# Head of an expert layer: token tile 0 ahead of tile 1, GpSimd out of the routing, weights in order of use, last norm's row by a broadcast load

## The chip, the cores and the metric

The kernel runs on one core of a Trainium2 chip. The metric is the time of one execution on the device in microseconds; the smaller is the better. Times are medians of repeated runs; the profile is of one execution, with its own time.

## The reference

A two-part network on 256 tokens of width 1024, all in float32. The first part has a pooling mixer, two gated feed-forward layers (width 2816) and a block attention of 16 heads. The second part is one hybrid layer: a modulation from a vector c (six rows: shift, scale, gain for the mixer and for the experts), a sparse attention and an RWKV branch that are mixed by sigmoid gates and projected by w_out, and then a mixture of experts. The change lies from the end of the mix on, which computes:

```python
x = x + g1 * (mixed @ w_out)
h2 = rms_norm(x, norm2_g) * (1 + sc2) + sh2
x = x + g2 * moe_ffn(h2, router_w, router_bias, exp_gate, exp_up, exp_down, sh_gate, sh_up, sh_down)
return rms_norm(x, final_g)
```

moe_ffn takes sigmoid scores of 64 experts per token, adds a bias for the choice, keeps the best 4 of 8 groups (by the sum of each group's two best), takes the best 8 experts in them, and weights them by their scores, normalised to a sum of 2.5. Each expert is a gated feed-forward of width 256; a shared expert of the same form runs on all tokens.

## The kernel before, in words

**Tiling.** The 256 tokens are two tiles of 128, called t = 0 and 1. The residual x_sb lies with tokens in the partitions. Sums over tokens by 1024 columns are built in four PSUM banks, accs[t][h], h being the half of 512 columns. [...]

**End of the mix** (lines 976 to 1025). `dense` runs the branch projections and the eight units of w_out. Each unit multiplies a split pair of operands (a high and a low part, three matmuls, `mm3` at line 205) into accs. The last `late` units (line 996, here two) are done for token tile 0 only, and `tail(h)` adds them for tile 1 afterwards, one half h at a time. `upd(t, h)` (line 1011) multiplies the sum by g1 and adds x_sb, two VectorE passes over 128x512, and ScalarE sums the squares. `rsq` (line 231) turns these into the norm's factor: two small VectorE operations and a power on GpSimd. From line 1018 on ScalarE, VectorE and TensorE run in the order in which the program is written (`manual_schedule`); GpSimd's and SyncE's order is set by the compiler's planner.

**Head of the experts** (`moe`, line 1351). `xnorm(t)` scales accs into xn, half on VectorE and half on ScalarE. TensorE transposes xn in eight 128x128 pieces for a tile, and VectorE (pieces 0 to 3) and ScalarE (4 to 7) write them with gain and shift to hT. The router's matmuls (line 1432) follow for both tiles, then one sigmoid, then `modrow(g2, 5)` (line 532), which spreads the gain row g2 over the partitions by eight matmuls and two ScalarE copies. xn is split into xH (ScalarE) and xL (GpSimd, line 1438). `shared_gu(jj)` (line 1444) is the shared expert's gate and up projection, 32 TensorE instructions, for one of two column halves; GpSimd multiplies the shared down weights by g2 (line 1452). Then VectorE routes, tile by tile (lines 1455 to 1479): maxima in groups, the groups' choice, the eight best, sel and the weights gw. From sel TensorE counts ranks (prk, lines 1482 to 1484), between shared_gu(0) and shared_gu(1).

**The loop over pairs of experts** (line 1645). 64 experts run as 32 pairs. Tokens are gathered by matmuls with one-hot matrices (`place`, `gather`, pxg), four experts at a time. For pair n: `gu(0)`, the first half of gate and up; `turn` of the pair before (transposing its activations to aT); `comb` of the pair before that (adding its result into accs); a part of the next gather; `gu(1)`; `act`; and `down(0)`, `down(1)` of the pair before. `down` multiplies by g2 on VectorE, rounds to yH on ScalarE, and keeps the rest in yL on VectorE. After the loop the last pair's turn, down and comb run, the squares are summed, and the final norm is written out.

**Weights.** All weights of `moe` go through a ring of NR = 18 slots of 1 MiB (`etile`), in three pools: ering1 (slots 0 to 8), ering2 (9 to 15), ering3 (16 and 17). A slot is reused when its last reader is done. A pair takes four slots for gate and up (`gload`) and two for down (`load_down`). xn and hT use the two slots of ering3 first, the shared gate, up and down slots 0 to 2. SyncE issues all these loads, one behind the other: its queue stands at a load whose slot isn't free. The row of the final norm takes a slot six pairs before the end (line 1648): a 4 KB load, spread to all partitions by matmuls (pbc, line 1654) and ScalarE copies.

**Pools.** The pool of the mix ("mix", g1row and temporaries) lies on the left side of SBUF among pools that close before ering3 and ering2 open.

Of the kernel before, what the change touches and what calls it, by code (L numbers as in the profile page):

```python
# [128 lines left out]
def build(ctx, tc, A, out, dbg=None):  # L129
# [680 lines left out]
    with ExitStack() as es:  # L810
# [169 lines left out]
        wk = open_pool(es, "mix")  # L980
# [15 lines left out]
        dn, tail = downs(A["w_out_2"][0], 8, lambda u: parts[u], accs, 2)  # L996
# [28 lines left out]
        upd(1, 1)  # L1025
    pa.close()
    ering3 = open_pool(ctx, "ering3", E3)
    ering2 = open_pool(ctx, "ering2", NR - E1 - E3)
    moe(ctx, nc, tc, A, out, x_sb, accs, xp, modrow, gcol, bcol, rt, K, ident, sm, ps,
# [321 lines left out]
def moe(ctx, nc, tc, A, out, x_sb, accs, xp, modrow, gcol, bcol, rt, K, ident, sm, ps,  # L1351
# [48 lines left out]
    with open_pool("route") as w2:  # L1400

        xns = etile(2, 1024, True)
        hT = etile(8, 256, True)
        xn = xns[:, 0, :], xns[:, 1, :]

        turned = lambda a: a.rearrange("n (p k) -> n k p", k=8)
        wide = lambda a, h: a.rearrange("n (k p) -> n k p", k=8)[:, :, 64 * h:64 * h + 64]
# [3 lines left out]
        def xnorm(t):  # L1411
            V.tensor_scalar(wide(xn[t], 0), turned(accs[t][0]), x2s[t], None, op0=OP.mult)
            S.activation(wide(xn[t], 1), turned(accs[t][1]), AF.Copy, scale=x2s[t])
        xnorm(0)
        x2s[1] = rsq(x2s[1], "n")
        xnorm(1)
        for t in range(2):
            for k4 in range(2):
                p = ps("pt")
                for kk in range(4):  # L1420
                    k = 4 * k4 + kk
                    PE.transpose(p[:, kk * 128:(kk + 1) * 128], xn[t][:, k * 128:(k + 1) * 128], ident)
                for kk in range(4):
                    k, c = 4 * k4 + kk, slice(kk * 128, (kk + 1) * 128)
                    if k4:
                        S.activation(hT[:, k, sl[t]], p[:, c], AF.Identity, scale=gc(k), bias=bc(k))
                    else:
                        V.tensor_scalar(hT[:, k, sl[t]], p[:, c], gc(k), bc(k), op0=OP.mult, op1=OP.add)
        p = ps("pr")
        for t in range(2):  # L1430
            for k in range(8):
                PE.matmul(p[:, t * 64:t * 64 + 64], hT[:, k, sl[t]], rtr[:, k, :], start=k == 0, stop=k == 7)
        S.activation(sc[:, :, 0, :], p[:, 0:128].rearrange("p (t e) -> p t e", t=2), AF.Sigmoid)
        V.tensor_tensor(sc[:, :, 1, :], sc[:, :, 0, :], rb[:, None, :].to_broadcast([128, 2, 64]), op=OP.add)
        modrow(g2, 5)
        for t in range(2):
            S.activation(xH[:, t, :], xn[t], AF.Copy)
            G.tensor_tensor(xL[:, t, :], xn[t], xH[:, t, :].bitcast(F32), op=OP.subtract)
# [5 lines left out]
        def shared_gu(jj):  # L1444
# [7 lines left out]
            G.tensor_tensor(down[:, jj, :], down[:, jj, :], g2, op=OP.mult)  # L1452
        shared_gu(0)
        sel = w2.tile([128, 2, 64], F32, name="sel")
        for t in range(2):
            s8 = w2.tile([128, 8, 8], F32, name="s8", bufs=2)
# [29 lines left out]
        V.scalar_tensor_tensor(rks.rearrange("p a b -> p (a b)"), p[:, 0:128], 1.0, sel.rearrange("p a b -> p (a b)"), op0=OP.add, op1=OP.mult)  # L1486

# [130 lines left out]
    for jj in range(2):  # L1618
        V.tensor_tensor(sa[:, jj, :], sa[:, jj, :], spg[jj][:, 256:512], op=OP.mult)
# [25 lines left out]
    for n in range(NE // 2):  # L1645
        g, i = divmod(n, NG // 2)
        more = g + 1 < NE // NG
        if n == NE // 2 - 6:
            fgt = etile(2, 1024)
            fg, frow = fgt[:, 0, :], fgt[0:1, 1, :]  # L1650
            DMA.dma_start(frow, A["final_g_2"][None, :])
# [126 lines left out]
```

## Time and profile before

| what | value |
|---|---|
| median of 3 runs | 1396.15 us (1391.35 to 1396.72) |
| profiled execution | 1396.91 us, span 1394.8 us |
| TensorE busy | 1338.2 us (96% of the span) |
| VectorE busy | 743.8 us (53%) |
| ScalarE busy | 548.3 us (39%) |
| GpSimd busy | 118.8 us (9%) |
| loads and stores | 361.38 MB, mean 259 GB/s |

The span is the profiled execution from its first to its last instruction; its own time has a few us around it. Engines are PE (TensorE), PEld (its weight loads, which overlap), DVE (VectorE), ACT (ScalarE), POOL (GpSimd) and SP (SyncE, which only issues loads here). [...] Busy shares are averages over parts with different limits; the part that the change touches begins at about 843 us of the span (the last branch projection is done), the pairs of experts run from 904 to about 1373, and the end follows.

### The profile page before, as it was taken

How to read it: one execution, taken by the hardware profiler on the slowest of the kernel's cores; microseconds unless marked ns; L12 is line 12 of the kernel's file. 1: busy time of each engine (PE TensorE's matmuls, PEld its weight loads, DVE VectorE, ACT ScalarE, POOL GpSimd, SP SyncE). 2: the span in 40 equal slices, each digit the busy share in tenths (PEclk: the TensorE clock that was granted, in tenths of full speed). 3: DMA queues.
4: the chain of work that ended last, by engine and by line, in shares of the span. 5: the costliest groups of instructions: out<-in, count | busy, mean ns of one | idle time of the engine just before them, and what ended most of it. 6: DMA issues, size and time to landing. Idle time of an engine off the chain costs nothing.

```text
span 1394.8 us, 22867 instructions
## 1 busy us (share of the span) xinstructions
PE 1338.2 (96%) x9151; PEld 1003.3 (72%) x9151; DVE 743.8 (53%) x1420; ACT 548.3 (39%) x1087; POOL 118.8 (9%) x158
## 2 busy tenths in 40 slices
PE   5999999999999998899999998899999999999996
PEld 4899997998799997789989888644545445445443
DVE  4656657565765555468777676533333343343333
ACT  4444445655544445365664543211221222222212
POOL 3010001000100002203342100300000000000000
PEclk9999999999999999899999998999999999999998
DMA  7887766652866646944411159499999999999993
GB/s 253 294 247 250 250 225 213 210 192 92 290 234 225 212 157 207 182 131 147 154 62 63 63 219 361 134 335 380 405 408 409 408 409 409 408 409 409 368 403 138
DMA packets 157312, 361.38 MB, mean 259 GB/s; under 512 B 9865, under 2 KB 92101, under 8 KB 153874
## 3 DMA queue, kind: packets, MB, share of 16 engines
q1 hardware_dynamic: 154674, 353.36, 70.0%
q0 software_dynamic: 2528, 6.51, 1.8%
q8 instruction: 75, 1.23, 0.4%
q14 instruction: 35, 0.29, 0.1%
HBM read 357.46 MB, written 2.37 MB: 258 GB/s over the span
## 4 chain that ended last, share of the span: by engine, by line
PE 79%; DMA 7%; issue 5%; DVE 5%; ACT 2%; POOL 1%; SPq 0%; POOLq 0%; ACTq 0%; DVEq 0%
PE pgu L1557 15%; PE pdn L1581 7%; PE pgu L206 5%; PE pgu L207 5%; PE pgu L208 5%; PE pxg L1524 4%; PE pz L206 4%; PE acc L1597 4%; PE pz L207 4%; PE pz L208 4%; PE acc L208 3%; PE acc L206 3%; PE acc L207 3%; DMA ew<-in_exp_up 3%; DMA raw<-in_w_gate_up 2%
## 5 line engine op out<-in xcount | busy, mean ns | idle before, releaser
L191 DVE TENSOR_TENSOR wL<-raw,wH 128x1024 fp32r<-128x1024 f32 (+1 forms) x229 | 270.7, 1186 | 200.2 <-ACT wH L190 199.4
L190 ACT ACTIVATE wH<-raw 128x1024 fp32r<-128x1024 f32 (+1 forms) x231 | 235.7, 1026 | 254.2 <-PE pgu L207 106.7
L207 PE MATMUL pgu<-hL,wH 128*128 128x256 f32 x704 | 198.1, 281 | 1.3 <-DVE hL L267 1.3
L206 PE MATMUL pgu<-hH,wH 128*128 128x256 f32 x704 | 198.0, 282 | 0.0
L208 PE MATMUL pgu<-hH,wL 128*128 128x256 f32 x704 | 198.0, 281 | 0.0
L207 PEld LDWEIGHTS pgu<-hL,wH 128*128 128x128 f32 x704 | 133.0, 189 | 3.5 <-DVE hL L267 1.7
L206 PEld LDWEIGHTS pgu<-hH,wH 128*128 128x128 f32 x704 | 132.7, 189 | 2.9 <-issue 0.6
L208 PEld LDWEIGHTS pgu<-hH,wL 128*128 128x128 f32 x704 | 133.0, 189 | 0.0
L206 PE MATMUL pz<-hH,wH 128*128 128x256 f32 x400 | 119.5, 299 | 3.3 <-ACT hH L190 2.6
L1557 PE MATMUL pgu<-ew,xx 128*64 128x512 f32 x512 | 117.8, 596 | 1.6 <-DMA ew<-in_exp_up 1.5
L1557 PE MATMUL pgu<-ew,xg 128*64 128x512 f32 x512 | 117.0, 596 | 0.4 <-DMA ew<-in_exp_up 0.4
L1581 PE MATMUL pdn<-ew,aT 128*64 128x512 f32 (+1 forms) x528 | 115.6, 580 | 0.0
L207 PE MATMUL pz<-hL,wH 128*128 128x256 f32 x400 | 114.3, 286 | 1.2 <-DVE hL L191 1.2
L208 PE MATMUL pz<-hH,wL 128*128 128x256 f32 x400 | 113.4, 284 | 0.0
L1581 PEld LDWEIGHTS pdn<-ew,aT 128*64 128x64 f32 x528 | 37.8, 137 | 72.1 <-issue 71.1
L1557 PEld LDWEIGHTS pgu<-ew,xx 128*64 128x64 f32 x512 | 36.2, 137 | 69.4 <-issue 66.1
L1557 PEld LDWEIGHTS pgu<-ew,xg 128*64 128x64 f32 x512 | 35.6, 137 | 67.4 <-issue 66.2
L1584 ACT ACTIVATE yH<-pdn 128x512 fp32r<-128x512 f32 (+1 forms) x66 | 38.5, 584 | 112.6 <-DVE pdn L1583 112.6
L206 PEld LDWEIGHTS pz<-hH,wH 128*128 128x128 f32 x400 | 76.6, 192 | 7.5 <-ACT hH L190 2.9
L207 PEld LDWEIGHTS pz<-hL,wH 128*128 128x128 f32 x400 | 76.7, 192 | 2.6 <-DVE hL L191 1.4
L208 PEld LDWEIGHTS pz<-hH,wL 128*128 128x128 f32 x400 | 76.6, 191 | 0.4 <-issue 0.3
L236 POOL TENSOR_TENSOR rstd<-ssv,mhalf 128x1 f32<-128x1 f32 x16 | 9.8, 614 | 768.0 <-DVE ssv L234 767.9
(408 smaller groups left out, 2528.1 us busy)
## 6 DMA issues: line engine op xcount, KB each, us to landing
ew<-in_exp_gate SPq DMA_DIRECT2D x128, 512.0 KB, 12.7
ew<-in_exp_up SPq DMA_DIRECT2D x128, 512.0 KB, 12.8
ew<-in_exp_down SPq DMA_DIRECT2D x64, 1024.0 KB, 12.1
raw<-in_w_gate_up SPq DMA_DIRECT2D x44, 1024.0 KB, 5.5
raw<-in_ada_w SPq DMA_DIRECT2D x24, 1024.0 KB, 5.0
raw<-in_w_in SPq DMA_DIRECT2D x23, 1024.0 KB, 5.3
raw<-in_w_down SPq DMA_DIRECT2D x22, 1024.0 KB, 5.3
raw<-in_w_kv SPq DMA_DIRECT2D x8, 1024.0 KB, 5.5
```

The source lines that it names most:

```text
L190: S.activation(dstH, src, AF.Copy)
L191: second.tensor_tensor(dstL, src, dstH.bitcast(F32), op=OP.subtract)
L206: PE.matmul(out_, lH, rH, start=first, stop=False)
L207: PE.matmul(out_, lH, rL, start=False, stop=False)
L208: PE.matmul(out_, lL, rH, start=False, stop=last)
L236: G.tensor_tensor(r, v, mhalf[:, 0:1], op=OP.pow)
L1524: PE.matmul(p[:, kk * w:kk * w + w], x[:, t, (kb + kk) * 128:(kb + kk) * 128 + 128], r, start=t == 0 and i == 0, stop=t == 1 and i == 1, s ...
L1557: PE.matmul(self.pg[64 * e:64 * e + 64, :].rearrange("p (i c) -> p i c", i=2), self.xg[:, k, 64 * e:64 * e + 64], self.W[e][k // 4][:, :, ...
L1581: PE.matmul(p[64 * e:64 * e + 64], self.aT[:, j, 64 * e:64 * e + 64], self.D[e][:, j, c:c + w], start=j == 0, stop=j == 1, skip_group_chec ...
L1584: S.activation(yH[:, sl], p, AF.Copy)
L1597: PE.matmul(self.ac[t][h][:, sl], l, self.y[h][i][:, sl], start=False, stop=i == 1 and self.last, skip_group_check=True)
```

## The change

- `late` is 4 instead of 2: four units of w_out are held back for token tile 1.
- The mix pool lies on the right side and closes after the last `upd`. ering3 opens earlier, xn is taken from it in `build`, and xnorm(0) runs ahead of upd(1, 1).
- In `moe`, token tile 0 is transposed, written to hT, and routed to its scores before tile 1 is transposed; modrow(g2, 5) stands ahead of the first router; the sigmoid runs tile by tile, as does the bias addition of the choice.
- xL is computed on VectorE after the ranks, and the shared down weights are multiplied by g2 on VectorE after `begin(0)`; both were GpSimd's.
- `load_down` of a pair is issued after the gate and up loads of the next pair.
- The final norm's row is loaded by one load that writes all 128 partitions, behind the last expert's weights; its matmuls and copies go.
- At the end, the last pair's turn stands between the two downs of the pair before, and its down(0) ahead of the older pair's combs; its down(1) comes ahead of its comb(0).

```diff
--- before.py
+++ after.py
@@ -977,7 +977,8 @@
         rt = open_pool(ctx, "router", side="right").tile([128, 576], F32, name="rt")
 
 
-        wk = open_pool(es, "mix")
+        mix = ctx.enter_context(ExitStack())
+        wk = open_pool(mix, "mix", side="right")
         g1 = wk.tile([128, D], F32, name="g1row")
         modrow(g1, 2)
         parts = {}
@@ -993,7 +994,7 @@
                     parts[2 * c + jj] = (mH[:, jj, :], mL[:, jj, :])
             return fin
         accs = []
-        dn, tail = downs(A["w_out_2"][0], 8, lambda u: parts[u], accs, 2)
+        dn, tail = downs(A["w_out_2"][0], 8, lambda u: parts[u], accs, 4)
         br = []
         wrb = loads(A["w_rwkv_br_2"][0], 4)
         for c in range(4):
@@ -1022,11 +1023,21 @@
         upd(1, 0)
         x2s[0] = rsq(x2s[0], "n")
         tail(1)
-        upd(1, 1)
+
+
     pa.close()
     ering3 = open_pool(ctx, "ering3", E3)
+    xn = ering3.tile([128, 2048], F32, tag="ew", name="ew").rearrange("p (t d) -> p t d", t=2)
+
+    def xnorm(t):
+        turned, wide = (lambda a: a.rearrange("n (p k) -> n k p", k=8)), xn[:, t, :].rearrange("n (k p) -> n k p", k=8)
+        V.tensor_scalar(wide[:, :, 0:64], turned(accs[t][0]), x2s[t], None, op0=OP.mult)
+        S.activation(wide[:, :, 64:128], turned(accs[t][1]), AF.Copy, scale=x2s[t])
+    xnorm(0)
+    upd(1, 1)
+    mix.close()
     ering2 = open_pool(ctx, "ering2", NR - E1 - E3)
-    moe(ctx, nc, tc, A, out, x_sb, accs, xp, modrow, gcol, bcol, rt, K, ident, sm, ps,
+    moe(ctx, nc, tc, A, out, accs, xn, xnorm, xp, modrow, gcol, bcol, rt, K, ident, sm, ps,
         x2s, order, rsq, hl, rows, bcast, ering1, ering2, ering3)
 
 
@@ -1348,7 +1359,7 @@
         yield
 
 
-def moe(ctx, nc, tc, A, out, x_sb, accs, xp, modrow, gcol, bcol, rt, K, ident, sm, ps,
+def moe(ctx, nc, tc, A, out, accs, xn, xnorm, xp, modrow, gcol, bcol, rt, K, ident, sm, ps,
         x2s, order, rsq, hl, rows, bcast, ering1, ering2, ering3):
     V, S, G, PE, DMA = nc.vector, nc.scalar, nc.gpsimd, nc.tensor, nc.sync
     NE, CAP, NG = 64, 64, 4
@@ -1398,44 +1409,42 @@
     bc = lambda k: bcol[:, 1, k:k + 1]
     g2 = mp.tile([128, D], F32, name="g2row")
     with open_pool("route") as w2:
-
-        xns = etile(2, 1024, True)
         hT = etile(8, 256, True)
-        xn = xns[:, 0, :], xns[:, 1, :]
-
-        turned = lambda a: a.rearrange("n (p k) -> n k p", k=8)
-        wide = lambda a, h: a.rearrange("n (k p) -> n k p", k=8)[:, :, 64 * h:64 * h + 64]
         sc = w2.tile([128, 2, 2, 64], F32, name="scn")
         sl = [slice(t * 128, (t + 1) * 128) for t in range(2)]
 
-        def xnorm(t):
-            V.tensor_scalar(wide(xn[t], 0), turned(accs[t][0]), x2s[t], None, op0=OP.mult)
-            S.activation(wide(xn[t], 1), turned(accs[t][1]), AF.Copy, scale=x2s[t])
-        xnorm(0)
+        def turns(t):
+
+            pt = [ps("pt") for _ in range(2)]
+            for k in range(8):
+                PE.transpose(pt[k // 4][:, k % 4 * 128:k % 4 * 128 + 128], xn[:, t, k * 128:(k + 1) * 128], ident)
+            return [p[:, kk * 128:(kk + 1) * 128] for p in pt for kk in range(4)]
+
+        def features(t, pt, ks):
+            for k in ks:
+                if k > 3:
+                    S.activation(hT[:, k, sl[t]], pt[k], AF.Identity, scale=gc(k), bias=bc(k))
+                else:
+                    V.tensor_scalar(hT[:, k, sl[t]], pt[k], gc(k), bc(k), op0=OP.mult, op1=OP.add)
+
+        def router(t):
+            p = ps("pr")
+            ks = (0, 4, 1, 5, 2, 6, 3, 7)
+            for k in ks:
+                PE.matmul(p[:, 0:64], hT[:, k, sl[t]], rtr[:, k, :], start=k == 0, stop=k == ks[-1])
+            S.activation(sc[:, t, 0, :], p[:, 0:64], AF.Sigmoid)
+
+        pt = turns(0)
+        features(0, pt, (0, 1, 4, 5, 6, 7))
         x2s[1] = rsq(x2s[1], "n")
+        features(0, pt, (2, 3))
         xnorm(1)
+        modrow(g2, 5)
+        router(0)
+        features(1, turns(1), range(8))
+        router(1)
         for t in range(2):
-            for k4 in range(2):
-                p = ps("pt")
-                for kk in range(4):
-                    k = 4 * k4 + kk
-                    PE.transpose(p[:, kk * 128:(kk + 1) * 128], xn[t][:, k * 128:(k + 1) * 128], ident)
-                for kk in range(4):
-                    k, c = 4 * k4 + kk, slice(kk * 128, (kk + 1) * 128)
-                    if k4:
-                        S.activation(hT[:, k, sl[t]], p[:, c], AF.Identity, scale=gc(k), bias=bc(k))
-                    else:
-                        V.tensor_scalar(hT[:, k, sl[t]], p[:, c], gc(k), bc(k), op0=OP.mult, op1=OP.add)
-        p = ps("pr")
-        for t in range(2):
-            for k in range(8):
-                PE.matmul(p[:, t * 64:t * 64 + 64], hT[:, k, sl[t]], rtr[:, k, :], start=k == 0, stop=k == 7)
-        S.activation(sc[:, :, 0, :], p[:, 0:128].rearrange("p (t e) -> p t e", t=2), AF.Sigmoid)
-        V.tensor_tensor(sc[:, :, 1, :], sc[:, :, 0, :], rb[:, None, :].to_broadcast([128, 2, 64]), op=OP.add)
-        modrow(g2, 5)
-        for t in range(2):
-            S.activation(xH[:, t, :], xn[t], AF.Copy)
-            G.tensor_tensor(xL[:, t, :], xn[t], xH[:, t, :].bitcast(F32), op=OP.subtract)
+            S.activation(xH[:, t, :], xn[:, t, :], AF.Copy)
 
         xx = xp.tile([128, 2, 8, 128], F32, name="xx", tag="x_sb")
         sa = xx[:, 0, 0:4, :].rearrange("p a b -> p (a b)").rearrange("p (j n) -> p j n", j=2)
@@ -1449,10 +1458,10 @@
                     PE.matmul(p[:, i * 256:(i + 1) * 256], w[:, k, jj * 128:(jj + 1) * 128], hT[:, k, :], start=k == 0, stop=k == 7,
                               skip_group_check=True)
             S.activation(sa[:, jj, :], p[:, 0:256], AF.Silu)
-            G.tensor_tensor(down[:, jj, :], down[:, jj, :], g2, op=OP.mult)
         shared_gu(0)
         sel = w2.tile([128, 2, 64], F32, name="sel")
         for t in range(2):
+            V.tensor_tensor(sc[:, t, 1, :], sc[:, t, 0, :], rb, op=OP.add)
             s8 = w2.tile([128, 8, 8], F32, name="s8", bufs=2)
             for g in range(8):
                 V.max(s8[:, g, :], sc[:, t, 1, g * 8:(g + 1) * 8])
@@ -1484,6 +1493,8 @@
         PE.matmul(p[:, 64:128], K("su"), sel[:, 1, :], start=False, stop=True)
         shared_gu(1)
         V.scalar_tensor_tensor(rks.rearrange("p a b -> p (a b)"), p[:, 0:128], 1.0, sel.rearrange("p a b -> p (a b)"), op0=OP.add, op1=OP.mult)
+        for t in range(2):
+            V.tensor_tensor(xL[:, t, :], xn[:, t, :], xH[:, t, :].bitcast(F32), op=OP.subtract)
 
     wk = ctx.enter_context(open_pool("moew"))
 
@@ -1616,6 +1627,7 @@
 
     begin(0)
     for jj in range(2):
+        V.tensor_tensor(down[:, jj, :], down[:, jj, :], g2, op=OP.mult)
         V.tensor_tensor(sa[:, jj, :], sa[:, jj, :], spg[jj][:, 256:512], op=OP.mult)
     half(0, 0)
     half(0, 1)
@@ -1645,17 +1657,10 @@
     for n in range(NE // 2):
         g, i = divmod(n, NG // 2)
         more = g + 1 < NE // NG
-        if n == NE // 2 - 6:
-            fgt = etile(2, 1024)
-            fg, frow = fgt[:, 0, :], fgt[0:1, 1, :]
-            DMA.dma_start(frow, A["final_g_2"][None, :])
-            for h in range(2):
-                p = ps("pbc")
-                PE.matmul(p, K("ones")[0:1, :], frow[:, h * 512:(h + 1) * 512], start=True, stop=True)
-                S.copy(fg[:, h * 512:(h + 1) * 512], p)
         pT, wsl = tiles[g]
         cur = Pair((2 * n, 2 * n + 1), spots[g % 2][:, i], pT[:, i, :], wsl[:, i:i + 1], accs, n > NE // 2 - 3)
-        cur.load_down()
+        if prev:
+            prev.load_down()
         if more and i == 0:
             begin(g + 1)
         cur.gu(0)
@@ -1672,14 +1677,20 @@
         cur.act()
         if prev:
             prev.down(0)
+            if n == NE // 2 - 1:
+                cur.turn()
             prev.down(1)
         old, prev = prev, cur
-    prev.turn()
+    prev.load_down()
+    fgt = etile(2, 1024)
+    fg, sq = fgt[:, 0, :], fgt[:, 1, :]
+    DMA.dma_start(fg, bcast(A["final_g_2"], D))
+    prev.down(0, 2)
     old.comb(0)
     old.comb(1)
     order.close()
     cnt = nc.values_load(mi[0:1, 0:1], min_val=0, max_val=T)
-    o, sq = etile(2, 1024), fgt[:, 1, :]
+    o = etile(2, 1024)
 
     def squares(t, h):
         S.activation(sq[:, h * 512:(h + 1) * 512], accs[t][h], AF.Square, accum_out=ss[t][:, h:h + 1])
@@ -1704,11 +1715,10 @@
     ss = [sm.tile([128, 2], F32, name="ss") for _ in range(2)]
     order = ctx.enter_context(ExitStack())
     order.enter_context(tc.manual_schedule(engines=MANUAL))
-    prev.down(0, 2)
+    prev.down(1, 2)
     prev.comb(0, 2)
     for t in range(2):
         squares(t, 0)
-    prev.down(1, 2)
     for t in range(2):
         gain(t)
     prev.comb(1, 2)
```

## Rows read from the trace of the kernel before

**Rows 1.** Busy by stretch: us, length, engines (x instructions), PEclk, DMA share, GB/s.

```profile
870.00:880.00 10.00, 9.25 (x48) 8.30 (x46) 9.31 (x36) 4.74 (x6) 7.35 (x4) 0.93 0.00 0
1100.00:1200.00 100.00, 100.00 (x515) 48.92 (x512) 38.25 (x73) 20.40 (x46) 0.00 (x0) 1.00 1.03 409
1300.00:1350.00 50.00, 49.59 (x249) 24.64 (x246) 17.41 (x32) 9.79 (x24) 0.00 (x0) 1.00 0.97 376
```

**Rows 2.** SyncE's queue: start, us, queue, line, operation.

```profile
857.85 0.34 SPq L1381 DMA_DIRECT2D ew<-in_exp_up  x1
881.94 0.33 SPq L1381 DMA_DIRECT2D ew<-in_exp_gate  x1
...
931.07 10.58 SPq L1366 DMA_DIRECT2D ew<-in_exp_down  x2
...
1307.57 9.64 SPq L1366 DMA_DIRECT2D ew<-in_exp_down  x2
...
1356.34 7.12 SPq L1366 DMA_DIRECT2D ew<-in_exp_down  x2
```

**Rows 3.** TensorE's timeline, head: start, us; in brackets idle before, releaser.

```profile
858.50 3.67 PE L1422 MATMUL pt<-k_base,ew 128*128 128x128 f32 x16 [3.79 <-ACT ew L1413]
861.96 6.93 PE L1432 MATMUL pr<-rt,ew 128*128 128x64 f32 x32
...
871.78 7.07 PE L1449 MATMUL pgu<-ew 128*128 128x256 f32 x32
...
882.87 0.69 PE L1484 MATMUL prk<-sel,k_base 128*128 128x64 f32 x2 [3.62 <-DVE sel L1474]
883.35 9.62 PE L1449 MATMUL pgu<-ew 128*128 128x256 f32 x32
...
904.14 3.65 PE L1557 MATMUL pgu<-ew,xg 128*64 128x512 f32 x16
```

**Rows 4.** VectorE's timeline, end of the mix and routing.

```profile
848.05 0.68 DVE L191 TENSOR_TENSOR mL<-mixt,mH 128x512 fp32r<-128x512 f32 x1
851.35 0.70 DVE L1013 TENSOR_TENSOR acc<-acc,g1row 128x512 f32<-128x512 f32 x1 [2.62 <-PE acc L208]
...
869.24 0.29 DVE L1434 TENSOR_TENSOR scn<-scn,rt 128x128 f32<-128x128 f32 x1 [6.51 <-ACT scn L1433]
...
872.83 2.22 DVE L1479 TENSOR_SCALAR gw<-gw,wr 128x64 f32<-128x64 f32 x1
...
883.31 0.25 DVE L1479 TENSOR_SCALAR gw<-gw,wr 128x64 f32<-128x64 f32 x1
```

**Rows 5.** GpSimd's timeline, routing.

```profile
872.65 4.67 POOL L1452 TENSOR_TENSOR ew<-ew,g2row 128x1024 f32<-128x1024 f32 x2 [13.72 <-ACT g2row L538]
```

**Rows 6.** Busy by stretch, TensorE alone: us, length, busy, PEclk, DMA, GB/s.

```profile
554.00:555.00 1.00, 0.00 (x0) 1.00 1.09 345
857.00:858.00 1.00, 0.00 (x0) 0.83 1.04 410
871.00:872.00 1.00, 1.00 (x8) 0.84 0.00 0
```

**Rows 7.** TensorE's timeline, an earlier pair of transposes.

```profile
555.06 1.06 PE L249 MATMUL pt<-k_base,xn 128*128 128x128 f32 x8 [1.66 <-DVE xn L773]
```

**Rows 8.** The chain that ended last, in the loop: start, us, what.

```profile
1281.73 1.91 PE pbc L1654 x4
```

**Rows 9.** TensorE's timeline, end of the loop.

```profile
1360.26 3.62 PE L1557 MATMUL pgu<-ew,xx 128*64 128x512 f32 x14 [1.52 <-DMA ew<-in_exp_up]
...
1369.50 3.60 PE L1581 MATMUL pdn<-ew,aT 128*64 128x512 f32 x16
```

**Rows 10.** The tile psrow: its load's time from issue to landing.

```profile
DMA to landing us min/median/max: 10.6/10.6/10.6
```

**Rows 11.** VectorE's timeline, the end.

```profile
1375.49 0.41 DVE L1570 COPY aT<-pat 128x256 f32<-128x256 f32 x1
...
1383.66 1.29 DVE L1688 TENSOR_TENSOR ew<-acc,ew 128x512 f32<-128x512 f32 x2
```

## The prediction

> **What bounds the kernel now.** I read the busy time by stretch first. The expert part, from 904 us on, shows two resources full at once: TensorE busy in all of 1100 to 1200, and the loads at 409 GB/s [rows 1]. One pair of experts is 6 MiB, 6.29 MB: at 409 GB/s that is 15.4 us, while TensorE takes (1369.5 - 904.1) / 32 = 14.5 us a pair [rows 3, 9]. The loads are the slower of the two, TensorE lives on what was loaded ahead, and at the last pair the lead is gone: it waits 1.52 us for in_exp_up [rows 9]. So there are two questions: when TensorE may begin pair 0, and how long the loads stand still before that.
>
> Ahead of it, 870 to 880 moves 0 GB/s [rows 1]: SyncE issued at 857.85 and then not until 881.94, because all 18 slots of the ring were taken [rows 2]. In that time TensorE ran the head. Its timeline shows two idle stretches, 3.79 us ahead of the transposes and 3.62 us ahead of prk, which waits for sel of VectorE; the transposes, the router and most of the second shared_gu ran at the lower clock level: the granted clock falls in 857 to 858 and is back in 871 to 872 [rows 6], and that second shared_gu took 9.62 us where the first took 7.07 for the same 32 pieces [rows 3]. VectorE's timeline says why sel was late: the same 128x64 operation of line 1479 took 2.22 us for tile 0 and 0.25 for tile 1; the long one ends with GpSimd's first 2.3 us instruction [rows 4, 5]. From line 1434 at 869.24 to sel of tile 1 it is 13.6 us. The chain of waits runs through all of this, so the head is on the path, the loads beside it.
>
> **The head, step by step** (clock of the run before). [...] Durations of steps 2 and 3 without a group are read from the timelines of VectorE, ScalarE and GpSimd between 851 and 872.
> 1. Held back are four units of token tile 1, not two, so token tile 0 has 12 pieces fewer before it. Fifteen pieces run between VectorE's start at 851.35 and TensorE's idle from 858.50 - 3.79 = 854.71, so one is 0.224 us, and the gain is at most 2.7 us. But units 6 and 7 need mL, which VectorE ends at 848.05 + 0.68 = 848.73 [rows 3, 4]; 7 pieces stand behind it, so accs[0][0] is ready at 850.3 and VectorE starts some 0.9 us earlier than before. Bounds 0 and 2.7, taken 0.9, by the mL row. TensorE stands some 1.8 us for it, and the longer tails end at 853.7 and 856.4.
> 2. upd(1, 0) waits on VectorE for the first tail, and rsq of tile 0 stands behind it: 853.8, two passes of 0.70, two small operations 0.4, GpSimd's power 0.55, xnorm(0) 0.75: the transposes begin at 857.3 instead of 858.50. upd(1, 1), before ahead of xnorm(0), now follows it.
> 3. Tile 1 follows on VectorE and ScalarE: two passes, the square 0.8, rsq with the power 1.0, xnorm 0.75, from 857.1 on: 861.6 with the two features that stand between. TensorE fills this with 8 transposes (1.06 in a row at the upper level, [rows 7]), modrow (16 pieces of the transposes' shape: 2.1, or the 3.67 of the lower level) and the router of tile 0 (half of 6.93 at the lower level; 1.7 to 3.5). Then 8 transposes, ScalarE's four features 1.5 (behind the two copies of g2, 1.2, which now stand ahead of the first sigmoid), router 1: it ends at 864.9, 4.0 us ahead of the run before (861.96 + 6.93). With everything from 857.3 on at the lower price (1.84, 3.67, 3.47, 1.84, 3.47) it ends at 871.6.
> 4. shared_gu(0) follows without a gap, 7.07: 872.0. Beside it VectorE routes. One tile costs 3.83 us without GpSimd (869.24 to 872.83 + 0.25), so two from 863.8 end at 871.5, and sel of tile 1 some 0.7 before: hidden behind shared_gu(0) by 1.2 us. Without that cover, every us over it is on the path.
> 5. prk 0.5, shared_gu(1) 7.07 instead of 9.62: 879.5. Behind prk VectorE now has xL (two of 128x1024, 1.4 each as twice the 0.70 of 128x512), pk and pw (four of 128x256, 0.4 each), two products down x g2 (1.4 each), two of sa: 8.3 us. The gather needs only xL and pk, 4.7 us after prk, inside shared_gu(1); down is needed 4 us after it. What left GpSimd is hidden.
> 6. From the end of shared_gu(1) to pair 0 nothing changes, 904.14 - 892.97 = 11.2. Pair 0 starts at 890.7.
>
> Head: 904.1 - 890.7 = **13.4 us** (6 to 15 with the bounds of steps 1 and 3).
>
> **The loads.** SyncE's queue is in order. W is a pair's four gate and up tiles, D its two down tiles. In the order before, D of a pair stands ahead of the next W, so a W that has a slot waits for a D that has none: at 931.07 a D held the queue 10.58 us [rows 2]. Afterwards the order is W0 W1 D0 W2 D1 W3. Again 13 MiB of experts fit before the ring is full, landed by 869. Slot by slot, each with 1 us of latency: xn frees at 875.1 (behind xL, now on VectorE; 881.94 before), so 7 us of standstill; hT at 879.5, 1.4 us; sh_down 3.4 us; the first W0 slots 1.2 us and 0.6. That is 13.6 us. The other 179 MiB, 187.7 MB, take 459 us at 409 GB/s: the last D lands at 869 + 13.6 + 459 = 1342. Before it was issued at 1363.5 [rows 2].
>
> TensorE needs 465.5 us less the waits from pair 0 to the end of the last gate and up, so until 1353, and the last D at about 1357. The loads are 15 us ahead: TensorE becomes the only bound, its 1.52 us wait goes. The final norm's row no longer sits in the loop: four pbc pieces, 1.91 us on the chain [rows 8], go; its slot no longer shortens the ring, which held D for 9.64 us at 1307.57 [rows 2]. The load is now 512 KB instead of 4 KB, behind the last D. A broadcast of that shape, psrow, landed 10.6 us after its issue [rows 10]; this one is first read some 20 us after it, so it costs nothing, and at twice psrow's time about 1 us. Loop: 1.5 + 1.9 = **3.4 us**.
>
> **The end.** Before, aT of the last pair waits on VectorE until 1375.49 [rows 11], behind both yL of the pair before, and down of the last pair begins at 1376.5 after the old combs. Now turn stands between the two downs: aT at 1373.6 (yL of half 0 is ahead of it), the second product 0.5 later, down(0) of the last pair at 1374.0, and the old combs fill TensorE while VectorE and ScalarE evacuate. The last yL comes at 1381.0 instead of 1383.7 (where line 1688 begins, [rows 11]); then ScalarE's four squares of 0.8 leave 2.4 of the 2.7. Bounds 0 and 3; taken **2.5 us**.
>
> Sum: 13.4 + 3.4 + 2.5 = 19.3. The profiled execution took 1396.91 (span 1394.8, 2.1 around it), so 1377.6; the median of the runs, 1396.15, lies 0.8 below. I forecast 1377.5.
>
> **The rivals.**
> *The clock falls in the head.* It fell at 857.8 after some 3 us without work, and stayed up across the 1.66 us gap ahead of the transposes at 555.06 [rows 6, 7]. My gaps in the head are under 1 us, except 1.3 us in step 1. Against: work between the gaps is small pieces, and before it did not bring the clock back from 858.5 to 871. If it falls at about 861, router 0, the second transposes and router 1 take 3.47 + 1.84 + 3.47 instead of 4.4, so 4.4 us more, and shared_gu(0) another 2.6 (as the second did, 9.62 - 7.07): 1384.5. [...]
> *The order on SyncE stays.* That queue is not in the hand-written order, so D may still go first. Then the loads end some 10 us later, 1352, just in time; only the last W is late, by what the loop gained: 1381. For it: the issue order of before already departs from the program's.
> *The loads stand in the new order (the slower side).* A D waits for a slot freed at the end of a pair's turn, and everything stands behind it, once a pair. TensorE needs the last D at 1357: that is 474 us for 187.7 MB, 396 GB/s. Below that the loads decide. At 376 GB/s, which 1300 to 1350 shows, they take 499 us and end 25 us late: 1402. It costs the whole gain from 381 GB/s down, where 1.1 us of standstill a pair is enough. Against: the 376 came with the ring short of a slot, and 409 holds otherwise. At 383 it would be 1393, no change.
>
> **How the numbers follow.** Forecast 0.68, its own range 1373 to 1381 (head 2 either way, end 1.5). Clock 0.15. Order stays 0.08. Standing loads 0.09, of which 0.05 end within 0.5% (7 us, about what a measurement of this kernel can tell from no change) and 0.04 slower. Faster 0.91. The range 1370 to 1387 takes in the clock and the order with their spread; the bounds of steps 1 and 3 (1376 to 1385) lie within it, and some 2 in 100 are left below it and 9 in 100, the standing loads, mostly above.
>
> **What would show it.** Transposes of tile 0 start 1 us or more after the end of the second tail at a clock of 1.00; no VectorE operation of the routing over 0.5 us; no idle TensorE ahead of prk; pair 0 starts 12 to 15 us earlier in the span; no TensorE wait for in_exp_up or in_exp_down; the last load well ahead of the end. The prediction is wrong if pair 0 starts less than 9 us earlier, or if TensorE waits for loads in the loop.

## The result, and the profile after

| what | before | after |
|---|---|---|
| median of 4 runs each, taken together | 1396.09 us (1391.35 to 1396.72) | 1374.66 us (1373.99 to 1375.76) |
| ratio, with its 95% interval | | 0.9855 (0.9832 to 0.9877) |
| profiled execution, span | 1396.91, 1394.8 us | 1375.12, 1373.0 us |
| TensorE busy | 1338.2 us | 1324.2 us |

The change makes the kernel 21.4 us faster; the forecast was 18.6 us (1377.5), and the time lies in its range. Three points split the difference of the two spans, 21.80 us: the start of pair 0, and the silus (ScalarE's activation, one a pair) of the first and of the last pair. Pair 0 starts 12.49 us earlier (904.14 to 891.65), the stretch between the silus is 6.87 us shorter, and what follows is 2.44 us shorter. The two silu rows of before, on ScalarE's timeline (start, us, and in brackets the idle time before):

```profile
913.61 0.38 ACT L1562 ACTIVATE es<-pgu 128x256 f32<-128x256 f32 x1 [3.60 <-issue]
...
1369.72 0.38 ACT L1562 ACTIVATE es<-pgu 128x256 f32<-128x256 f32 x1 [10.36 <-PE pgu L1557]
```

The same rows after. The length between them is 456.11 before and 449.24 after:

```profile
901.12 0.38 ACT L1573 ACTIVATE es<-pgu 128x256 f32<-128x256 f32 x1 [3.60 <-issue]
...
1350.36 0.38 ACT L1573 ACTIVATE es<-pgu 128x256 f32<-128x256 f32 x1 [7.55 <-PE pgu L1568]
```

TensorE's timeline of the head after, to be laid beside [rows 3]. The 3.79 us gap ahead of the transposes is 1.09, prk follows without one, and both shared_gu (L1458) take 7.13:

```profile
857.64 1.06 PE L1420 MATMUL pt<-k_base,ew 128*128 128x128 f32 x8 [1.09 <-DVE ew L1034]
858.54 1.95 PE L537 MATMUL pbc<-k_base,mods 128*128 128x128 f32 x16
860.74 2.00 PE L1434 MATMUL pr<-rt,ew 128*128 128x64 f32 x16 [0.25 <-DVE ew L1428]
862.58 1.04 PE L1420 MATMUL pt<-k_base,ew 128*128 128x128 f32 x8
863.78 2.16 PE L1434 MATMUL pr<-rt,ew 128*128 128x64 f32 x16 [0.16 <-DVE ew L1428]
865.78 7.13 PE L1458 MATMUL pgu<-ew 128*128 128x256 f32 x32
872.75 0.33 PE L1491 MATMUL prk<-sel,k_base 128*128 128x64 f32 x2
...
873.36 7.13 PE L1458 MATMUL pgu<-ew 128*128 128x256 f32 x32
...
891.65 3.65 PE L1568 MATMUL pgu<-ew,xg 128*64 128x512 f32 x16
```

The clock by stretch, TensorE alone. PEclk, the column behind the busy time, is the granted share of the full clock; in the heads that were read it is 1.00, the upper level, or 0.50, the lower, and a value between where it changes within the stretch. [rows 6] had 0.83 and 0.84; here it stays at 1.00.

```profile
857.00:858.00 1.00, 0.36 (x4) 1.00 1.02 410
871.00:872.00 1.00, 1.00 (x6) 1.00 0.00 0
```

VectorE's timeline, beside [rows 4]. sel of tile 1 is ready at 871.21, 1.5 us ahead of prk, and the last operation of the routing takes 0.25, as it does for tile 0 at 868.03:

```profile
849.48 0.69 DVE L191 TENSOR_TENSOR mL<-mixt,mH 128x512 fp32r<-128x512 f32 x1
851.68 0.70 DVE L1014 TENSOR_TENSOR acc<-acc,g1row 128x512 f32<-128x512 f32 x1 [1.52 <-PE acc L208]
...
871.01 0.20 DVE L1483 TENSOR_SCALAR sel<-mc 128x64 f32<-128x64 f32 x1
...
871.71 0.25 DVE L1488 TENSOR_SCALAR gw<-gw,wr 128x64 f32<-128x64 f32 x1
```

Busy by stretch (all engines), beside [rows 1]: loads run again before 880, and TensorE has no idle time left in 1300 to 1350.

```profile
870.00:880.00 10.00, 10.00 (x51) 8.89 (x50) 8.16 (x20) 0.38 (x1) 3.66 (x5) 1.00 0.28 91
1300.00:1350.00 50.00, 50.00 (x248) 22.68 (x246) 15.82 (x29) 8.16 (x18) 0.00 (x0) 1.00 0.98 391
```

SyncE's queue, beside [rows 2]: the standstill of the head is 859.17 to 876.22, the last expert loads go out at 1332.42, and the row of the final norm (L1687) behind them; it took 15.2 us to land and was first read at 1362.39.

```profile
859.17 0.43 SPq L1392 DMA_DIRECT2D ew<-in_exp_up  x1
876.22 0.33 SPq L1392 DMA_DIRECT2D ew<-in_exp_gate  x1
...
1332.42 4.20 SPq L1377 DMA_DIRECT2D ew<-in_exp_down  x4
1337.53 0.34 SPq L1687 DMA_DIRECT2D ew<-in_final_g  x1
```

### The profile page after: what moved, and what is told of

Read it like the earlier page. It is cut to its first block, busy times and chain, and to the rows that moved or that the text cites. A ratio compares the mean times of both kernels' runs of the same rounds, so it can differ in the third digit from the quotient of the medians.

```text
span 1373.0 us, 22938 instructions
## 1 busy us (share of the span) xinstructions
PE 1324.2 (96%) x9147; PEld 993.1 (72%) x9147; DVE 741.6 (54%) x1425; ACT 547.8 (40%) x1086; POOL 110.9 (8%) x154
## 3 DMA queue, kind: packets, MB, share of 16 engines
q8 instruction: 75, 1.23, 0.4%
## 4 chain that ended last, share of the span: by engine, by line
PE 82%; issue 5%; DMA 5%; DVE 4%; ACT 2%; POOL 1%; SPq 1%; POOLq 0%; ACTq 0%; DVEq 0%
PE pgu L1568 16%; PE pdn L1592 8%; PE pgu L206 6%; PE pgu L207 6%; PE pgu L208 6%; PE pxg L1535 4%; PE acc L1608 4%; PE pz L206 4%; PE pz L207 4%; PE pz L208 4%; PE acc L208 3%; PE acc L206 3%; PE acc L207 3%; DMA raw<-in_w_gate_up 2%; DMA gain_scr<-bcol 1%
## 5 line engine op out<-in xcount | busy, mean ns | idle before, releaser
L208 PE MATMUL acc<-wH,aL 128*128 128x512 f32 x176 | 69.9, 398 | 1.7 <-DVE aL L191 1.4
## 6 DMA issues: line engine op xcount, KB each, us to landing
ew<-in_exp_up SPq DMA_DIRECT2D x128, 512.0 KB, 12.8
```

Source lines behind the costliest of these rows:

```text
L208: PE.matmul(out_, lL, rH, start=False, stop=last)
```

## The experiments

Each edit is of the changed kernel, but for the two that say before. Heads are from mL's start to pair 0 (56.09 us before, 42.17 after): what lies ahead of mL differs from execution to execution. Loops are from the first silu to the last, ends from there to the end of the span, which is read to 0.1 us; in the kernels whose end and loads are the changed one's they spread over 22.49 to 23.00. Ratios are against runs of the kernel before on the same chip.

| edit | median us | ratio (95%) | head | loop | end |
|---|---|---|---|---|---|
| changed kernel again | 1374.67 | 0.9873 (0.9857 to 0.9889) | 42.18 | 449.24 | 22.49 |
| GpSimd back | 1381.03 | 0.9897 (0.9869 to 0.9925) | 47.33 | 449.24 | 22.91 |
| two units held back | 1377.28 | 0.9863 (0.9836 to 0.9891) | 44.58 | 449.24 | 23.00 |
| three units held back | 1374.61 | 0.9866 (0.985 to 0.9883) | 42.32 | 449.24 | 22.94 |
| tiles together | 1383.03 | 0.9902 (0.987 to 0.9933) | 49.70 | 449.24 | 22.96 |
| before, GpSimd out | 1388.20 | 0.994 (0.9916 to 0.9964) | 46.00 | 456.06 | 25.06 |
| load order back | 1380.24 | 0.9884 (0.9859 to 0.9908) | 42.18 | 453.46 | 23.19 |
| norm row back | 1378.70 | 0.9882 (0.9854 to 0.991) | 42.19 | 451.37 | 23.95 |
| both back | 1383.03 | 0.9905 (0.988 to 0.993) | 42.18 | 456.11 | 23.38 |
| before, new load order | 1390.45 | 0.9959 (0.9946 to 0.9973) | 51.48 | 451.42 | 25.81 |
| old end | 1377.82 | 0.9896 (0.9879 to 0.9912) | 42.17 | 449.24 | 24.84 |

**GpSimd back into the routing.**

```diff
+            G.tensor_tensor(xL[:, t, :], xn[:, t, :], xH[:, t, :].bitcast(F32), op=OP.subtract)
...
+            G.tensor_tensor(down[:, jj, :], down[:, jj, :], g2, op=OP.mult)
...
-            V.tensor_tensor(xL[:, t, :], xn[:, t, :], xH[:, t, :].bitcast(F32), op=OP.subtract)
...
-        V.tensor_tensor(down[:, jj, :], down[:, jj, :], g2, op=OP.mult)
```

> The changed kernel with xL and the product of the shared down weights back on GpSimd during the routing. My theory: GpSimd's four instructions of 2.3 us hold up the two-input operations of VectorE's routing again, sel of tile 1 comes 4 to 6 us later than 871.2, TensorE stands 3 to 4 us ahead of prk after the first shared_gu has ended at 872.9, the clock falls there, the second shared_gu takes 9.6 us instead of 7.1: pair 0 starts 4 to 7 us later than 891.65 and the time grows by as much. Rival, the order of the token tiles alone brought the gain and the first shared_gu covers a slow routing as well: 0 to 1.5 us.

The head grew by 5.16 us. GpSimd's timeline, two instructions to a row, and then VectorE's while it routes tile 0:

```profile
863.01 4.68 POOL L1462 TENSOR_TENSOR ew<-ew,g2row 128x1024 f32<-128x1024 f32 x2 [1.95 <-DMA ew<-in_exp_gate]
867.64 4.67 POOL L1448 TENSOR_TENSOR xn2L<-ew,xn2H 128x1024 fp32r<-128x1024 f32 x2
```

```profile
864.89 0.56 DVE L1466 TENSOR_TENSOR scn<-scn,rt 128x64 f32<-128x64 f32 x1
...
866.20 1.53 DVE L1472 TENSOR_TENSOR gs<-s 128x8 f32<-128x8 f32 x1
...
868.37 1.66 DVE L1478 TENSOR_SCALAR pen<-gs 128x8 f32<-128x8 f32 x1
870.07 2.33 DVE L1480 TENSOR_TENSOR mc<-scn,pen 128x64 f32<-128x64 f32 x1
```

For tile 1, when GpSimd is done, the same four take 0.22, 0.17, 0.17 and 0.23: 5.3 us are lost in them, nearly all of the head's 5.16. The last ends at 872.40, the last of GpSimd's instructions at 872.31. TensorE's timeline then has the gap ahead of prk again, and the shared_gu behind it starts at a granted clock of 0.50:

```profile
876.95 0.69 PE L1495 MATMUL prk<-sel,k_base 128*128 128x64 f32 x2 [3.03 <-DVE sel L1485]
877.43 8.57 PE L1459 MATMUL pgu<-ew 128*128 128x256 f32 x32
```

**GpSimd out of the kernel before**, the same edit the other way round.

```diff
-            G.tensor_tensor(xL[:, t, :], xn[t], xH[:, t, :].bitcast(F32), op=OP.subtract)
...
+            V.tensor_tensor(xL[:, t, :], xn[t], xH[:, t, :].bitcast(F32), op=OP.subtract)
```

> The kernel before with one part of the change alone: xL on VectorE behind the ranks, the product of the shared down weights on VectorE behind the first placement. My theory: the routing takes 7.5 us instead of 13.6, sel of tile 1 is there before the first shared_gu ends, TensorE has no gap ahead of prk (4.0 us) and its clock stays up for the second shared_gu (2.5 us): pair 0 starts 6.5 us earlier, the time falls by 6.5 us. Rival, the routing is held up by something else than GpSimd: no change.

The head shrank by 10.1 us, more than expected. Of it 3.62 are the gap ahead of prk and 2.50 the second shared_gu (7.12). Another 3.6 lie ahead of the first shared_gu, where GpSimd does nothing: from the first transpose to it took 13.28 us before [rows 3] and 9.72 here, because the clock is back in 862 to 863 (0.75, then 1.00), not in 871 to 872. TensorE's timeline of that run:

```profile
857.17 3.67 PE L1422 MATMUL pt<-k_base,ew 128*128 128x128 f32 x16 [3.79 <-ACT ew L1413]
860.64 4.58 PE L1432 MATMUL pr<-rt,ew 128*128 128x64 f32 x32
```

That this belongs to the single execution and not to GpSimd shows in the kernel before with the new load order alone (below): its GpSimd is in, and the stretch took 8.82. Less these 3.6 the head shrank by 6.5, as expected. The loop stayed at 456.06 although pair 0 started 11.4 us earlier in the span: an earlier head alone does not use up the lead of the loads.

**Tiles together in `moe`**, as before.

```diff
-        pt = turns(0)
-        features(0, pt, (0, 1, 4, 5, 6, 7))
         x2s[1] = rsq(x2s[1], "n")
-        features(0, pt, (2, 3))
         xnorm(1)
+        for t in range(2):
+            features(t, turns(t), range(8))
+        for t in range(2):
+            router(t)
         modrow(g2, 5)
-        router(0)
-        features(1, turns(1), range(8))
-        router(1)
```

> The changed kernel with both token tiles transposed before either goes through the router, and modrow of g2 behind both routers, as before the change; xnorm of tile 0 stays ahead of the last upd. My theory: TensorE idles 2 to 3 us between the transposes of tile 0 and those of tile 1, modrow no longer fills a wait (1.95 us on the path), so the first shared_gu starts 2 to 3 us later than 865.8 with the clock up, and 6 to 9 us later if the clock falls in that gap. Rival, the order of the tiles is hidden beside the routing: less than 1 us.

The head grew by 7.53 us in the profiled execution, the slowest of this kernel's four (1380.6 to 1387.0). TensorE waits 2.91 us for tile 1, the granted clock falls in 863 to 864 (0.69, then 0.50) and is back in 877 to 878 (0.98), and transposes, routers and modrow run at the lower level until then:

```profile
865.57 1.94 PE L1420 MATMUL pt<-k_base,ew 128*128 128x128 f32 x8 [2.91 <-DVE ew L1034]
867.30 6.93 PE L1434 MATMUL pr<-rt,ew 128*128 128x64 f32 x32
```

**Two units of w_out held back**, as before, and **three**: `accs, 4)` becomes `accs, 2)` and `accs, 3)` in the call of `downs`.

> The changed kernel with two units held back for token tile 1 instead of four. My theory: accs of tile 0 are ready 0.9 us later (the stall for mL is what four units lose against), everything behind follows 0.9 us later, and TensorE now idles some 2.5 us ahead of the transposes instead of 1.1; if the clock holds the time grows by 0.9 us. Rival, four units are there to keep TensorE at work: the clock falls at that gap and the head loses another 4 to 8 us.

> The changed kernel with three units of w_out held back for token tile 1 instead of four. Held back two (the run before this one) cost 2.4 us in the head: VectorE's first pass of upd 3.49 us after mL's start instead of 2.20, then a 2.50 us gap of TensorE and the lower clock for some 3 us. Theory (step 1 of the forecast: mL sets the start of the first upd, so pieces are worth something only as far as they lie behind mL; 12 pieces of 0.224 us are 2.7 us and gained 1.3, so 1.4 us of them had slack): the 6 pieces of the third unit, 1.34 us, lie in that slack, upd starts 2.2 to 2.4 us after mL's start, the gap ahead of the transposes stays at 1.1 to 1.3, the clock stays up, head 42.2 to 42.5, time within 0.7 us of the changed kernel. Rival (each unit counts the same): upd 2.85 us after mL's start, a gap of 1.8 us, head 42.8 with the clock up and 43.4 or more with it down, time 0.7 to 1.5 us above the changed kernel.

With two, upd starts 3.49 us after mL's start instead of 2.20, so 1.29 us are the pieces; the other 1.1 of the 2.41 are the clock, which falls right behind the gap, in 860 to 861 (0.80, then 0.50), and is back in 864 to 865 (0.99). Neither theory had this size: the clock did fall, but for 3.4 us only:

```profile
860.26 1.63 PE L1420 MATMUL pt<-k_base,ew 128*128 128x128 f32 x8 [2.50 <-DVE ew L1034]
```

With three, upd starts 2.21 us after mL (VectorE, L1014), the gap is 1.23, and behind it the eight transposes take 1.06 and modrow 1.95, as in the changed kernel at 1.00: three units do all that four do, as mL sets the start.

**The order of the loads back**, **the norm's row back**, **both**, and **the new order alone in the kernel before**. The order's edit, then the row's:

```diff
-        if prev:
-            prev.load_down()
+        cur.load_down()
...
-    prev.load_down()
```

```diff
+        if n == NE // 2 - 6:
+            fgt = etile(2, 1024)
+            fg, frow = fgt[:, 0, :], fgt[0:1, 1, :]
+            DMA.dma_start(frow, A["final_g_2"][None, :])
+            ...
...
-    DMA.dma_start(fg, bcast(A["final_g_2"], D))
...
```

> The changed kernel with the old order of the loads alone: a pair's down weights issued with its gate and up weights, not behind those of the next pair. From the activation of pair 0 to that of pair 31 the changed kernel takes 449.2 us, the one before 456.1. My theory: the old order brings part of the waits back, at pair 31 above all, because the loads end some 8 us later and the last gate and up weights stand behind them: 0.3 to 3 us more in the loop. Rival, TensorE is the only bound and the order is of no account: loop 449.2. Second rival, the order alone is behind all waits of the kernel before: loop 454, 4.8 us more.

> The changed kernel with the last norm's row loaded as 4 KB six pairs before the end and spread by matmuls, as before the change; the new order of loads stays. My theory: TensorE pays the four pieces, 1.9 to 2.1 us in the loop at pair 26, and no wait for weights, since in the order of use the gate and up weights don't stand behind down weights: loop 451.3 us. Rival, the slot that the row holds delays the loads enough: waits at pairs 29 to 31 as before, loop 454 to 456.

> The changed kernel with both back: the old order of the loads and the last norm's row in the loop. My theory: the loop takes 456.1 us as in the kernel before, the early start of pair 0 changes nothing in it because the loads restart as much earlier: 6.9 us more than the changed kernel. Rival, the loads ended on a fixed date before: then the loop stretches by the head's gain, to 465 us and more.

> The kernel before with the new order of the loads alone. My theory: the waits of pairs 29 to 31 go and the row's pieces stay: loop 451.3 us instead of 456.1, the time falls by 4.8 us. Rival, the ring is short of a slot by the row and the loads end as late as before: 0 to 2 us.

The order costs 4.22 us in the loop (the theory had 0.3 to 3, its second rival 4.8), the row 2.13, both 6.87, the whole of the loop's difference: 0.52 come only with both. With both the loop is 456.11 again although pair 0 starts 12.5 us earlier, so the loads of the kernel before did not end on a fixed date. Undoing any other part does not move the loop. Of the row's 2.13, 2.03 stand at one pair (16.61 from silu to silu instead of 14.58), where pbc runs. The order's stand at the last five pairs (0.10, 0.36, 0.80, 0.35 and 2.62 us longer). There TensorE's timeline shows one wait, 1.43, and beside it two pieces that last 1.04 where the same two take 0.60 in the changed kernel:

```profile
1344.04 1.04 PE L1568 MATMUL pgu<-ew,xx 128*64 128x512 f32 x2
1346.51 3.65 PE L1568 MATMUL pgu<-ew,xx 128*64 128x512 f32 x14 [1.43 <-DMA ew<-in_exp_up]
```

The wait ends with the landing of the up load that was issued at 1333.69 and took 12.8 us. The last up load goes out at 1341.37 in this kernel and at 1331.10 in the changed one.

The row also goes with an end of 23.95. Its kernel issues the last down loads until 1346.9, the changed one until 1336.6, and TensorE's timeline behind the last silu shows what that costs. The first products of down, in the changed kernel and then with the row back:

```profile
1350.14 1.89 PE L1592 MATMUL pdn<-ew,aT 128*64 128x512 f32 x8
```

```profile
1352.14 2.82 PE L1592 MATMUL pdn<-ew,aT 128*64 128x512 f32 x8
```

With the row the second of the two down weights that they read lands at 1352.99, after they began; so the row, which takes a slot of the ring, costs some 1 us in the end besides its pieces in the loop.

The new order alone in the kernel before did what it did in the changed one (451.42 and, with the row in both, 451.37). In both kernels with the new order and the row SyncE stands some 15 to 16 us late in the loop, which the changed kernel does not, and TensorE waits there for no gate or up weights. The price comes at the end: in the kernel before with the new order the end is 25.81, with the old one 25.06. SyncE's queue of that run:

```profile
1297.66 0.34 SPq L1381 DMA_DIRECT2D ew<-in_exp_up  x1
1313.79 0.33 SPq L1381 DMA_DIRECT2D ew<-in_exp_gate  x1
```

**The old end.**

```diff
-            if n == NE // 2 - 1:
-                cur.turn()
...
-    prev.down(0, 2)
+    prev.turn()
...
-    prev.down(1, 2)
+    prev.down(0, 2)
...
+    prev.down(1, 2)
```

> The changed kernel with the old order of the end alone: the last pair's turn behind both downs of the pair before, its down(0) behind the older pair's combs, its down(1) behind its comb(0). Theory (the end is a term of its own, worth 2.5 us as forecast, 2.44 as the two traces have it): from the last pair's silu to the end of the span 25.1 us (22.64 in the changed kernel), aT of the last pair 0.7 us later or more because it waits behind both yL; from the first to the last silu of the loop 449.2, from mL's start to pair 0 42.2, both as in the changed kernel; time 2.4 us above the changed kernel. Rival (the end got shorter because the loads no longer land late, not by its order): the end stays within 0.5 us of 22.64 and the time within 0.7 us.

The end took 24.84, 2.20 us more than in the changed kernel, and 1.8 more than the longest (23.00) of the kernels that keep its end and its loads; head and loop did not move. VectorE's timeline has aT 5.77 us after the last silu (1349.76), in the changed kernel 3.95 (1354.31):

```profile
1355.53 0.41 DVE L1581 COPY aT<-pat 128x256 f32<-128x256 f32 x1
```

**The changed kernel again.**

> The changed kernel again, beside the two others, on the same chip. Both theories: 1374.0 to 1376.0, head 42.2 from mL's start to pair 0, loop 449.2 from the first silu to the last, end 22.6. Rival: a head that differs from the first profile by more than 1 us, or a clock that falls in it, which would say that the head's clock is a matter of the single run.

It came out the same in every part. Against the seven runs of the kernel before on this chip (median 1392.71) the gain is 18.0 us, not 21.4: the median of the kernel before lies between 1392.7 and 1397.2 in the four sets of runs, that of the changed one at 1374.7 in both of its sets. None of the kernels is faster than the changed one beyond the runs' spread.

## Why the prediction was right, and where its sizes were off

The mechanisms were right and the sum came out 2.5 us short in spans (19.3 for 21.80). The 1377.5 is that sum taken from the profiled execution; taken from the median of 1396.15 it gives 1376.9. By its parts:

| term | forecast | measured |
|---|---|---|
| head, pair 0 in the span | 13.4 | 12.49 |
| loop, wait for in_exp_up | 1.5 | 4.74 (6.87 less the row's 2.13) |
| loop, norm row | 1.9 | 2.13 |
| end | 2.5 | 2.44 |

**The mis-sized term is the wait in the loop.** The forecast took the one bracket of 1.52 us [rows 9] for the whole price of late loads. Pair by pair, the kernel before loses 1.45, 0.52 and 2.84 us at the last three pairs, 4.8 in all. The bracket holds only a part. The run with the old order settles it: one bracket of 1.43 and 4.22 us lost, and beside the bracket two pieces that look long instead of late (1.04 for 0.60).

**Steps 1 and 2.** upd starts 2.20 us after mL's start instead of 3.30: 1.1 for the 0.9 taken, and as step 1 says mL sets it (three units do the same as four). But TensorE's stand of 1.8 us did not come, the first tail was there when VectorE was, and the transposes began 8.16 us after mL's start, where the forecast's times make 9.25. (The terms of step 2 as written add up to 856.9, not to its 857.3.)

**Steps 3 to 6.** Router 1 ends 16.46 us after mL's start (forecast 16.85). sel is covered by 1.5 us (1.2). The second shared_gu takes 7.13 (7.07), and from its end to pair 0 it is 11.2, as forecast. From mL on the head gained 13.92 us, for the 13.4 forecast; 1.43 of it does not reach the span, because mL itself started that much later in the profiled execution after. Of this 0.24 is the change's own: from the first piece of modrow(g1, 2), the matmuls that spread g1 ahead of the mix, to mL it is 32.25 to 32.27 us in the three traces of the kernel before and its edits, and 32.49 to 32.51 in the ten of the changed one and its edits. The rest lies ahead of that, where the two programs are the same; mL starts between 846.7 and 851.2 in the other executions but the one of the tiles together (853.4).

**The head by its parts.** Undone one at a time, GpSimd costs 5.16, the units 2.41 and the tiles together 7.53, in sum 15.1 for a head of 13.92: the parts share the clock's price, and each by itself brings a gap back (3.03, 2.50 and 2.91 us) and with it the lower level, 0.50. Where xnorm(0) stands, ahead of the last upd, was left as it is in all of these edits, so its part is not known. The saving of the whole against [rows 3] also holds some luck of the single execution: with the same 3.79 us gap, the clock came back after 13 us in the profile of before, and after 5.3 and 3.5 us in the two edits of that kernel (in the second it is 0.50 in 862 to 863 and 1.00 in 864 to 865), where the heads were 46.00 and 51.48. The second of these has the head of the kernel before unchanged, so some 4.6 us of the 13.92, and of the forecast that was read from the same profile, hang on how late the clock came back in it.

**The rivals.** The clock did not fall in the head: three idle times (1.09, 0.25 and 0.16 us within 8 us) left it at 1.00, in every microsecond from 853 to 886. The order on SyncE did not stay, and when it was put back by hand the time was 1380.2, near the 1381 of that rival. The loads did not stand. But their lead was far smaller than the 15 us forecast. The last down load, forecast to land at 1342 and to be read at 1357, was issued at 1336.25, took 15.2 us to land (1351.45) and was read from 1354.84 on: a lead of 3.4 us. The last up load, issued at 1331.10, landed 10.2 us later, 5.4 us ahead of the last half of gate and up at 1346.66. The standstill at the head was longer than the 13.6 us taken: 870 to 880 moved 91 GB/s and 880 to 1300 moved 400, which against 409 is 7.8 and 9.2 us, 17 in all. That is 3.4 of the 9.4 us by which the last landing was late; the rest stays open. The 1 us taken for each slot is near what the kernel before shows for one: xL, the last reader of xn, ends at 881.91, 881 to 882 moved 0 GB/s, and 882 to 883 moved 25.

**The end.** VectorE has aT at 1354.31, ahead of the second product and yL, as forecast, and the products with the norm's row (L1699) start at 1362.39, 12.03 us after the last silu; before (L1688, [rows 11]) it was 13.94. On VectorE's timeline:

```profile
1354.31 0.42 DVE L1581 COPY aT<-pat 128x256 f32<-128x256 f32 x1
...
1362.39 1.41 DVE L1699 TENSOR_TENSOR ew<-acc,ew 128x512 f32<-128x512 f32 x2 [0.31 <-ACT ew L1696]
```

## What to carry to other kernels

Price a wait in a loop by the distance from one iteration to the next at the same instruction, against the undisturbed distance, and not by the idle bracket of one row: here 4.8 us stood behind 1.5. A gap of TensorE cost itself and what ran at the lower clock behind it: with the tiles together the gap is 2.91 us and the head 7.53 longer. So work that fills such a gap (the other half of the tokens, a broadcast that is due anyway) gains more than the gap's length; behind the gap of 1.09 the clock stayed at 1.00. An engine that is busy 9% of the time can still be on the critical path, by holding up another engine in its few busy microseconds: GpSimd's 9.3 us beside the routing cost the head 5.16.

## What the runs showed of the hardware that was not expected

**The return of the clock is not a constant.** In the heads where it was read, the granted clock fell to 0.50 after every gap of 2.50 to 3.79 us. After work resumed it came back in 3.4 us (GpSimd back), 3.5 (before, new load order), 3.8 (two units), 5.3 (before, GpSimd out), 11.5 (tiles together), and 12.8 and 5.5 (the two gaps of the kernel before); what decides between them stays open. The longest gap, 4.66 us ahead of prk in the kernel before with the new load order, has a second shared_gu of 8.41 us behind it where the first took 7.07; if the 1.3 us were lost at half speed, the clock came back after some 3.1 us, an estimate. After gaps of 1.09 and 1.10 us it stayed at 1.00. The kernel before with its two gaps spreads over 1390.7 to 1400.4 us in all its runs; the changed kernel, whose longest gap in the head is 1.09, over 1374.0 to 1375.8 in eight. That the clock makes this spread was not shown: with three units held back the head is 42.32 as well, and four runs spread over 1372.6 to 1377.4.

**GpSimd's copies last longer beside VectorE's xL as well.** They took 0.49 and less before; beside xL, now on VectorE from 873.77 to 876.16, the first two take longer. GpSimd's timeline after:

```profile
874.00 1.09 POOL L1644 COPY both<-rks 128x64 f32<-128x64 f32 x1 [13.32 <-DVE rks L1495]
875.03 1.23 POOL L1645 COPY both<-gw 128x64 f32<-128x64 f32 x1
876.19 0.44 POOL L1644 COPY both<-rks 128x64 f32<-128x64 f32 x1
```

They end at 875.09 and 876.26, each some 0.1 us behind one of VectorE's two operations of 1.2 us. In the run with GpSimd back, where xL is GpSimd's, the same two take 0.49 and 0.43, and VectorE is the one that takes longer, 2.33 us for 0.23. There a TENSOR_SCALAR with one input tile was held too (1.66 us for 0.17), so what was held there is not the two-input operations alone.
